# Weight sums of two seven-product block multiplications, built in HBM scratch by copies and accumulating DMAs

## The chip, the cores and the metric

One core of a Trainium2 chip runs the whole kernel. The metric is the device time of the program in microseconds (us), median of several runs. The profile is of one execution of the same program; its times are counted from the start of its span.

## The reference

One decoder layer on x (256 tokens, 2048 columns), float32. A combined projection `x @ w_in` gives latent queries, a latent key/value, gates, an indexer and a recurrent input. Branch A is sparse attention, branch B a gated linear recurrence (RG-LRU); each is gated and projected, then merged:

```
branch_a = (attn * silu(attn_gate)) @ w_branch_a
branch_b = (h * silu(rnn_gate)) @ w_branch_b
merged   = sigmoid(x @ w_gA) * branch_a + sigmoid(x @ w_gB) * branch_b
out      = layernorm(ALPHA * x + merged @ w_out) * g + b
```

All matrix products are float32. The kernel makes each from three products of a split pair: a value v is kept as hi (v rounded to the matmul's float32r) and lo = v - hi, and hi·hi + hi·lo + lo·hi is summed in PSUM.

## The kernel before

**Order of work.** `col_jobs()` lists column jobs in time order: index queries (qi), attention gates (ag), 32 query tiles (q), merge gate chunks ga and branch A chunks ba, recurrent inputs (xr), merge gate chunks gb, recurrent gates (rg). A chunk of 512 columns has 16 ticks, any other job 4. The hand-written list `TAIL` gives the rest: pieces of the branch B product (bb), of the output product (o), and steps t1, t2, t3. A tick is the unit of the kernel's own agenda: generators spawned at a tick (`spawn(t, gen)`) emit their next instructions there and name the number of ticks to the next turn. The order of emission is the order of each engine's queue; nothing is reordered later. `D0` is the tick of the first query job, `C0` that of the first recurrent input, `B0` the start of the tail.

**Weights.** All weight pieces are listed in `halves`, in the order of use. `load_to(n)` issues the loads up to piece n on SP's queue, each into a tile `raw` of 128x1024 float32 (a ring of 4). `split_to(n)` turns pieces into hi on ScalarE (`hi_of`, L151) and lo on VectorE (`lo_of`, L155), each a ring of 5. PE reads hi and lo. Loads are emitted about nine pieces ahead of use, splits about five.

**Seven-product steps.** In some places a 2x2 block product is made with seven block products instead of eight, which needs sums of weight blocks and of input blocks. Three such places exist:

- j (steps j1 to j4, beside the query jobs): two other column blocks; its sums stay as they are.
- s (steps s1 and s2, 8 each, inside the chunks ba 1, ba 2 and ba 3): the last column block of the first merge gate and the first of the second. Weight quarters 11, 12, 21, 22 are of 8 rows (k) of 128x512 each.
- t (steps t1, 4 of them, t2 and t3 in the tail): part of branch B's first two column blocks, quarters of 4 rows each.

Before the change the weight sums of s and t are made on VectorE, piece by piece: `load_to` fetches the pair of quarters of a row into one raw tile and a third quarter into a tile `form[k]` (s) or `t2` (t, which lies in the place of the first half of the normalised input `xs`, once that is no more needed). `sums(i)` and `split_to` then subtract: for s1a and t1a the lines 309 and 312 or 311, for s1b and t1b line 338, for s2a line 352, for t2 line 308. The pieces s1b, s2b and t1b have no raw tile of their own: they read what s1a and s2a left in theirs, or `form` and `t2`.

The input `xs` is kept as two tiles of half the rows behind a small class `Rows`, so that `t2` and later the merged rows (`m0`) can take the place of the first.

Other work on the queues that matters here: SP also loads the attention bias tiles (`load_bias`, from HBM scratch `dz`, L621), POOL adds the mask to them (L625), makes the late input sums of j (`late_sum`, L1017 to L1019) and issues its own DMAs: the copies `dz <- dv` of 1 MB from HBM to HBM (L612) and loads of input rows into `form` tiles (L949).

Of the kernel before, what the change touches and what calls it, by code (L numbers as in the profile page):

```python
# [11 lines left out]
F32 = mybir.dt.float32  # L12
# [81 lines left out]


def quarters(i):

    steps = [("j1", k) for k in range(8)] + [("j2", k) for k in range(8)]  # L100
    steps += [("j3", k) for k in range(4)] + [("j4", k) for k in range(8)]
    return steps[:1] if i == 3 else steps[i - 4:i - 3] if i > 4 else []


def ticks(job):

    return 16 if job[0] in CHUNKS else 4


class Rows:  # L110

    def __init__(self, parts):
        self.parts = parts

    def __getitem__(self, key):
        p, k, c = key
        if isinstance(k, slice):
            e = k.start // (KT // 2)
            return self.parts[e][p, k.start - e * (KT // 2):k.stop - e * (KT // 2), c]
        return self.parts[k // (KT // 2)][p, k % (KT // 2), c]  # L120


@with_exitstack
def layer(ctx, tc, ar, out):
# [89 lines left out]
    nc8 = const.tile([P, 16], F32, name="nc8")  # L214
    xs = Rows([big.tile([P, KT // 2, 2 * T], F32R, name=f"xs{e}", tag=f"xs{e}", bufs=1) for e in range(2)])
    dv = dram.tile([NH, VL], F32, name="dv")
# [26 lines left out]
    NZ = len(halves)  # L243
    halves += [("wo", 3, pc) for pc in range(8)]
    raws, parts = {}, {}
    st = {"load": 0, "split": 0}

    def load_to(n):
        while st["load"] < min(n, len(halves)):
            i = st["load"]  # L250
            kind, a, s = halves[i]
            st["load"] += 1
            if kind in ("s1b", "s2b", "t1b") or kind in ("j2", "j4") and a % 2:
                continue
            if kind == "s1a":
                nc.sync.dma_start(form[a], ar["wgb"][0, 4 + a // 2, :, a % 2, :])
            if kind == "t1a":
                if a == 0:
                    t2.append(big.tile([P, KT // 2, 2 * T], F32, name="t2", tag="xs0", bufs=1))
                nc.sync.dma_start(t2[0][:, a, :], ar["wbb"][1, (Q + a) // 2, :, (Q + a) % 2, :])  # L260
            raw = wpool.tile([P, 1024], F32, name=f"raw{i}", tag="raw", bufs=4)
            raws[i] = raw
            if kind == "t2":
                nc.sync.dma_start(raw[:, :512], ar["wbb"][0, (Q + a) // 2, :, (Q + a) % 2, :])
                continue
            if kind == "wt":
                src = ar["wt"][a, :, s * 8:(s + 1) * 8, :].rearrange("p k c -> p (k c)")
            elif kind == "j1":
                src = ar["wj"][a].rearrange("p k c -> p (k c)")
            elif kind in ("j2", "j3", "j4"):  # L270
                src = {"j2": ar["wgb"][3, 4 + a // 2], "j3": ar["wga"][2, a], "j4": ar["wga"][2, 4 + a // 2]}[kind]
                src = src.rearrange("p k c -> p (k c)")
            elif kind in ("s1a", "s2a"):
                src = ar["ws"][a + (8 if kind == "s2a" else 0)].rearrange("p k c -> p (k c)")
            elif kind == "t1a":
                src = ar["wbp"][a].rearrange("p k c -> p (k c)")
            elif kind == "t3":
                src = ar["wbb"][1, Q // 2 + a].rearrange("p k c -> p (k c)")
            else:
                src = ar[kind][a, s].rearrange("p k c -> p (k c)")  # L280
            nc.sync.dma_start(raw, src)
# [3 lines left out]
    form = {}  # L285
    t2 = []

    def sums(i):


        kind, k, _ = halves[i]
        if kind in ("j2", "j4") and k % 2:
            i = next(n for n in reversed(range(i)) if halves[n][:2] == (kind, k - 1))
        raw = raws[i]
        half = raw[:, k % 2 * 512:(k % 2 + 1) * 512]
        if kind == "j1":
            return nc.vector.tensor_sub(form[k], raw[:, 512:], raw[:, :512])
        if kind == "j2":
            return nc.vector.tensor_sub(form[k], half, form[k])
        if kind == "j3":  # L300
            for e in range(2):
                c = slice(e * 512, (e + 1) * 512)
                nc.vector.tensor_sub(raw[:, c], form[2 * k + e], raw[:, c])
            return
        if kind == "j4":
            return nc.vector.tensor_sub(form[k], form[k], half)
        if kind == "t2":
            return nc.vector.tensor_sub(raw[:, 512:], raw[:, :512], t2[0][:, k, :])
        nc.vector.tensor_sub(raw[:, 512:], raw[:, 512:], raw[:, :512])
        if kind == "t1a":  # L310
            return nc.vector.tensor_sub(t2[0][:, k, :], t2[0][:, k, :], raw[:, 512:])
        nc.vector.tensor_sub(form[k], form[k], raw[:, 512:])

    def split_to(n):
        while st["split"] < min(n, len(halves)):
            i = st["split"]
            kind, k, _ = halves[i]
            follower = halves[i + 1][0] if i + 1 < len(halves) else None
            if follower in ("s1a", "t1a"):
                load_to(i + 2)  # L320
                sums(i + 1)
            load_to(i + 1)
# [11 lines left out]
            else:  # L334
                if kind in ("s1b", "t1b"):
                    raw = raws.pop(i - 1)
                    v2 = form[k] if kind == "s1b" else t2[0][:, k, :]
                    nc.vector.tensor_sub(raw[:, 512:], v2, raw[:, :512])
                    src = [(slice(0, 512), v2), (slice(512, 1024), raw[:, 512:])]
                elif kind == "j1":  # L340
                    src = [(slice(0, 512), raws.pop(i)[:, :512]), (slice(512, 1024), form[k])]
                elif kind in ("j2", "j4"):
                    n = i if k % 2 == 0 else next(n for n in reversed(range(i)) if halves[n][:2] == (kind, k - 1))
                    raw = raws.pop(n) if k % 2 else raws[n]
                    src = [(slice(0, 512), raw[:, k % 2 * 512:(k % 2 + 1) * 512]), (slice(512, 1024), form[k])]
                elif kind == "s2b":
                    src = [(slice(0, 512), form[k])]
                else:
                    raw = raws[i] if kind in ("s1a", "t1a") else raws.pop(i)
                    src = [(slice(0, 1024), raw)]  # L350
                if kind == "s2a":
                    nc.vector.tensor_sub(form[k], form[k], raw[:, :512])
                hi = wpool.tile([P, 1024], F32R, name=f"hi{i}", tag="hi", bufs=5)
# [5 lines left out]
                parts[i] = (hi, lo)  # L359
            if follower in ("j1", "j2", "j3", "j4", "t2"):  # L360
                load_to(i + 2)
# [411 lines left out]
    def post_bb(i, pss):  # L773
# [10 lines left out]
        yield TURN[i]  # L784
        if i == 0:
            xs.parts[0] = big.tile([P, KT // 2, 2 * T], F32R, name="m0", tag="xs0", bufs=1)
        gs = [gates.pop(("gb", i, t)) for t in range(2)]
# [172 lines left out]
    def quarter_sums():  # L960
# [8 lines left out]
        for j in range(4):  # L969
# [4 lines left out]
                 for i, (tag, bufs) in enumerate((("g", 2), ("g", 2), ("u", 2), ("r", 3)))]  # L974
            nc.vector.tensor_add(v[0], a21, a22)
            nc.vector.tensor_sub(v[2], a11, a21)
            nc.vector.tensor_sub(v[1], v[0], a11)
            nc.vector.tensor_sub(v[3], a12, v[1])
            yield
# [146 lines left out]
    def after_s1():  # L1126
# [6 lines left out]
        yield  # L1133
        nc.vector.tensor_add(c22, ps7[5], u3)
        nc.vector.tensor_add(u4, ps7[5], u4)
        ps7["u"] = u1, u3, u4, c22

    def after_s2():

        u1, u3, u4, c22 = ps7["u"]  # L1140
        nc.vector.tensor_add(u1, ps7[2], u1)
        nc.vector.tensor_sub(u3, u3, ps7[4])
        for t in range(2):
# [11 lines left out]
    def branch_sums():  # L1155

        SB.update((i, sp.tile([P, 2, Q, P], F32R, name=f"sb{i}", tag="s", bufs=4)) for i in range(1, 5))
        for e in range(0, Q, 4):
# [3 lines left out]
            x = {1: v[:, b, P:], 2: v[:, a, :P], 3: v[:, a, P:], 4: v[:, b, :P]}  # L1162
            nc.vector.tensor_add(x[1], x[3], x[1])
            nc.vector.tensor_sub(x[3], x[2], x[3])
            yield
            nc.vector.tensor_sub(x[2], x[1], x[2])
            nc.vector.tensor_sub(x[4], x[4], x[2])
            yield
# [72 lines left out]
    def after_t1():  # L1241
# [8 lines left out]
        yield  # L1250
        nc.vector.tensor_add(u4, psb[5], u3)
        nc.vector.tensor_add(u2, psb[5], u2)
        spawn(t_now[0] + 8, load_norm(0))
# [5 lines left out]

    D0, C0, G0 = at["q", 0], at["xr", 0], at["gb", 1]  # L1260
    spawn(D0 - 30, early_sums())
    for j, t in enumerate((76, 79, 83, 87)):
# [335 lines left out]
def lay_out(x, w_in, kv_norm_g, w_uv, w_branch_a, conv_w, conv_b, w_gate_a, b_gate_a,  # L1598
# [14 lines left out]
    for kind, m in (("ga", w[:, O_GA:O_GA + DM]), ("gb", w[:, O_GB:O_GB + DM]),  # L1613
# [3 lines left out]
                         w[:, O_GB:O_GB + 512].reshape(KT, P, 512)], axis=2)  # L1617
    ar["wbp"] = w_branch_b[0, :Q * P].reshape(Q, P, 4, 512)[:, :, :2]
    ar["wj"] = np.stack([w[:DM // 2, O_GA + 2 * 512:O_GA + 3 * 512].reshape(KT // 2, P, 512),
# [27 lines left out]
```

## Time and profile before

| | |
|---|---|
| median of 3 runs | 1011.74 us (1011.54 to 1012.13) |
| the profiled execution, time | 1012.71 us |
| its span | 1010.9 us |
| mean granted TensorE clock | 0.998 |
| HBM read, written | 208.01 MB, 6.32 MB |

Each part of the profile is read so: busy time of an engine is the union of its instructions; a group of instructions has its count and minimum, median and maximum duration in ns; "idle before" and "waited for" name the event that came last before an engine went on. "q" behind an engine's name (SPq) is its queue of waits and DMA issues. "To landing" is the time from the issue of a DMA until its completion was signalled.

### The profile page before, as it was taken

Reading aid. Unit: us, or ns where it says so; the run is one execution under the profiler, and the core shown is the slowest. Engines: PE = TensorE matmul, PEld = TensorE weight load, DVE = VectorE, ACT = ScalarE, POOL = GpSimd, SP = SyncE. Lnnn points to the kernel's source line nnn. Section 1 sums busy time; section 2 is a strip of 40 time slices with the busy share of each in tenths; the row PEclk is TensorE's granted clock in tenths of the full one; section 3 lists DMA queues with packets and bytes.
Section 4 is the critical chain, followed back from the end, with each engine's and each line's share of the span. In section 5 each row is a group of like instructions: output and inputs, shape, how many; then the busy total and the mean of one; then the engine's idle time right before and its main releaser. Section 6 shows DMA issues by size and latency. Waiting matters only on the chain.

```text
span 1010.9 us, 15117 instructions
## 1 busy us (share of the span) xinstructions
PE 1002.9 (99%) x5308; PEld 864.7 (86%) x5308; DVE 810.5 (80%) x1340; ACT 605.5 (60%) x1037; POOL 153.0 (15%) x188
## 2 busy tenths in 40 slices
PE   9999999999999999999999999999999999999997
PEld 8888888888888888888888888888888888888885
DVE  5678789778789988868888878888678997978685
ACT  5566656666766576566455555555885555644452
POOL 0015621111123310210000000000343320001002
PEclk9999999999999999999999999999999999999999
DMA  9846886766656665766676776556556668667752
GB/s 301 264 150 196 282 324 198 234 216 197 188 157 208 198 201 164 231 210 208 206 232 204 213 233 190 186 191 198 172 180 191 190 198 289 205 201 264 226 173 84
DMA packets 65132, 211.14 MB, mean 209 GB/s; under 512 B 7184, under 2 KB 14224, under 8 KB 64288
## 3 DMA queue, kind: packets, MB, share of 16 engines
q1 hardware_dynamic: 61376, 196.37, 61.2%
q0 software_dynamic: 2960, 12.88, 3.6%
q8 instruction: 42, 0.69, 0.3%
q10 hardware_dynamic: 720, 0.92, 0.3%
q14 instruction: 34, 0.28, 0.1%
HBM read 208.01 MB, written 6.32 MB: 212 GB/s over the span
## 4 chain that ended last, share of the span: by engine, by line
PE 94%; DVE 3%; ACT 1%; issue 1%; DMA 1%; DVEq 0%; ACTq 0%
PE ps_q L368 17%; PE ps_ag L368 9%; PE ps_rg L368 9%; PE ps_xr L368 9%; PE ps_ba L1293 3%; PE ps_ba L1292 3%; PE ps_ba L1294 3%; PE psq L368 2%; PE ps_qi L368 2%; PE ps_o L1193 2%; PE ps_o L1191 2%; PE ps_o L1190 2%; PE ps_bb L1191 2%; PE ps_bb L1193 2%; PE ps_bb L1190 2%; PE ps_ga L1292 1%
## 5 line engine op out<-in xcount | busy, mean ns | idle before, releaser
L155 DVE TENSOR_TENSOR lo<-raw,hi 128x1024 fp32r<-128x1024 f32 (+1 forms) x354 | 420.0, 1194 | 154.4 <-ACT hi L151 150.3
L151 ACT ACTIVATE hi<-raw 128x1024 fp32r<-128x1024 f32 (+1 forms) x354 | 352.3, 1012 | 148.3 <-PE ps_q L368 16.7
L368 PE MATMUL ps_q<-xs,hi 128*128 128x512 f32 x512 | 126.9, 391 | 0.0
L368 PEld LDWEIGHTS ps_q<-xs,hi 128*128 128x128 f32 x512 | 94.0, 188 | 18.4
L368 PEld LDWEIGHTS ps_q<-xs,lo 128*128 128x128 f32 x512 | 65.6, 191 | 2.5
L368 PE MATMUL ps_q<-xs,lo 128*128 128x256 f32 x512 | 66.4, 283 | 0.0
L625 POOL TENSOR_TENSOR bias<-bias,mask 128x256 f32<-128x256 f32 (+1 forms) x32 | 33.0, 1050 | 195.4 <-DMA bias<-dz 182.7
L368 PE MATMUL ps_ag<-xs,hi 128*128 128x512 f32 x256 | 60.1, 391 | 0.0
L368 PE MATMUL ps_rg<-xs,hi 128*128 128x512 f32 x256 | 59.5, 390 | 0.0
L368 PE MATMUL ps_xr<-xs,hi 128*128 128x512 f32 x256 | 59.5, 390 | 0.0
L368 PEld LDWEIGHTS ps_xr<-xs,hi 128*128 128x128 f32 x256 | 47.6, 188 | 9.6
L368 PEld LDWEIGHTS ps_rg<-xs,hi 128*128 128x128 f32 x256 | 47.6, 188 | 9.6
L368 PEld LDWEIGHTS ps_ag<-xs,hi 128*128 128x128 f32 x256 | 47.5, 188 | 9.6
L1293 PE MATMUL ps_ba<-lo,ua 128*128 128x512 f32 x128 | 49.9, 389 | 0.0
L1294 PE MATMUL ps_ba<-hi,ua 128*128 128x512 f32 x128 | 49.8, 389 | 0.0
L1292 PE MATMUL ps_ba<-hi,ua 128*128 128x512 f32 x128 | 49.8, 389 | 0.0
L151 ACT ACTIVATE hi<-form 128x512 fp32r<-128x512 f32 x40 | 25.3, 633 | 28.8 <-PE ps_ba L1294 8.9
L1190 PE MATMUL ps_bb<-hi,ub 128*128 128x512 f32 x104 | 41.1, 395 | 0.0
L1193 PE MATMUL ps_bb<-hi,ub 128*128 128x512 f32 x104 | 40.6, 390 | 0.0
L1191 PE MATMUL ps_bb<-lo,ub 128*128 128x512 f32 x104 | 40.6, 390 | 0.0
L850 POOL MEMSET xp<- 128x3 f32 x16 | 1.5, 100 | 253.3 <-ACT ga L1150 163.9
L368 PE MATMUL ps_ag<-xs,lo 128*128 128x256 f32 x256 | 32.9, 283 | 0.0
(456 smaller groups left out, 2198.4 us busy)
## 6 DMA issues: line engine op xcount, KB each, us to landing
raw<-in_wt SPq DMA_DIRECT2D x168, 512.0 KB, 4.6
raw<-in_wba SPq DMA_DIRECT2D x32, 512.0 KB, 3.8
raw<-in_wo SPq DMA_DIRECT2D x32, 512.0 KB, 4.4
raw<-in_wbb SPq DMA_DIRECT2D x26, 512.0 KB, 4.2
raw<-in_wga SPq DMA_DIRECT2D x24, 512.0 KB, 4.5
raw<-in_wgb SPq DMA_DIRECT2D x20, 512.0 KB, 4.8
raw<-in_ws SPq DMA_DIRECT2D x16, 512.0 KB, 4.2
wr<-in_wA SPq DMA_DIRECT2D x14, 424.0 KB, 5.0
```

The source lines that it names most:

```text
L151: nc.scalar.activation(hi, src, AF.Copy)
L155: nc.vector.tensor_sub(lo, src, f(hi))
L368: nc.tensor.matmul(ps[:, :n], w, rhs[:, :n], start=start, stop=stop)
L625: nc.gpsimd.tensor_add(b[:, r, :W[r]], b[:, r, :W[r]], mask[:, r, :W[r]])
L850: nc.gpsimd.memset(xp[:, 0:3], 0.0)
L1190: nc.tensor.matmul(o, mh, hi, start=left[t] == left_of[key][t], stop=False)
L1191: nc.tensor.matmul(o, mh, lo, start=False, stop=False)
L1193: nc.tensor.matmul(o, ml, hi, start=False, stop=left[t] == 0)
L1292: nc.tensor.matmul(o, mh, hi, start=first and d == 0, stop=False)
L1293: nc.tensor.matmul(o, mh, lo, start=False, stop=False)
L1294: nc.tensor.matmul(o, ml, hi, start=False, stop=d == KT - 1)
```

## The change

The sums of s and t are made in HBM before they are needed. A generator `weight_sums` emits for each of four sums t1 = 11 (+) 12, t3 = 12 (+) 22, t2 = 11 (+) t3, t4 = 21 (+) t2 and each block of four rows one copy of the first operand into a scratch tile of 1 MB, on SP's queue, and one accumulating DMA of the second operand onto it, from POOL. Copy and add of one tile are two turns of nine ticks apart. The sums have plus signs only, so input sums and the final additions turn signs to match (an add for a subtract and the other way round, same number of instructions). The pieces s1a, s1b, s2a, s2b, t1a, t1b and t2 are then plain loads of one or two quarters of 256 KB, each into a raw tile of its own. `form` is no more loaded with weights for s, the tiles `t2` and `m0` go, and `xs` is one tile. The array `wbp` holds twice the rows.

```diff
+ROWS = 4
+PAIRS = {"s": "ws", "t": "wbp"}
+OPERANDS = {"s1a": ("11", "t1"), "s1b": ("t2", "t3"), "s2a": ("21", "22"), "s2b": ("t4",),
+            "t1a": ("11", "t1"), "t1b": ("t2", "t3"), "t2": ("21", "t4")}
...
-    xs = Rows([big.tile([P, KT // 2, 2 * T], F32R, name=f"xs{e}", tag=f"xs{e}", bufs=1) for e in range(2)])
+    xs = big.tile([P, KT, 2 * T], F32R, name="xs")
...
+    depth = {"s": KT // 2, "t": Q}
+    summed = {}
+
+    def quarter(p, n, k):
+        if n[0] == "t":
+            return summed[p, n, k // ROWS][:, k % ROWS, :]
+        return ar[PAIRS[p]][depth[p] * (n[0] == "2") + k, :, int(n[1]) - 1, :]
+
+    def several(p, n, k):
+        if n[0] == "t":
+            return summed[p, n, k]
+        r = depth[p] * (n[0] == "2") + ROWS * k
+        return ar[PAIRS[p]][r:r + ROWS, :, int(n[1]) - 1, :].rearrange("k p c -> p k c")
+
+    def weight_sums(p, gap):
+
+        begun = []
+        for n, first, second in (("t1", "11", "12"), ("t3", "12", "22"), ("t2", "11", "t3"), ("t4", "21", "t2")):
+            for k in range(depth[p] // ROWS):
+                d = summed[p, n, k] = dram.tile([P, ROWS, 512], F32, name=f"sum_{p}{n}_{k}")
+                nc.sync.dma_start(d, several(p, first, k))
+                begun.append((d, several(p, second, k)))
+                yield gap
+                if len(begun) > 1:
+                    add_rows(*begun.pop(0))
+        add_rows(*begun.pop())
+
+    def add_rows(d, src):
+
+        nc.gpsimd.dma_start(d, src, accum_op=OP.add, max_dma_last_dim=8192)
...
-            if kind in ("s1b", "s2b", "t1b") or kind in ("j2", "j4") and a % 2:
+            if kind in ("j2", "j4") and a % 2:
                 continue
-            if kind == "s1a":
-                nc.sync.dma_start(form[a], ar["wgb"][0, 4 + a // 2, :, a % 2, :])
...
-            if kind == "t2":
-                nc.sync.dma_start(raw[:, :512], ar["wbb"][0, (Q + a) // 2, :, (Q + a) % 2, :])
+            if kind in OPERANDS:
+                for e, part in enumerate(OPERANDS[kind]):
+                    nc.sync.dma_start(raw[:, e * 512:(e + 1) * 512], quarter(kind[0], part, a))
                 continue
...
-        if kind == "t2":
-            return nc.vector.tensor_sub(raw[:, 512:], raw[:, :512], t2[0][:, k, :])
-        nc.vector.tensor_sub(raw[:, 512:], raw[:, 512:], raw[:, :512])
-        if kind == "t1a":
-            return nc.vector.tensor_sub(t2[0][:, k, :], t2[0][:, k, :], raw[:, 512:])
-        nc.vector.tensor_sub(form[k], form[k], raw[:, 512:])
...
-                if kind in ("s1b", "t1b"):
-                    raw = raws.pop(i - 1)
-                    v2 = form[k] if kind == "s1b" else t2[0][:, k, :]
-                    nc.vector.tensor_sub(raw[:, 512:], v2, raw[:, :512])
-                    src = [(slice(0, 512), v2), (slice(512, 1024), raw[:, 512:])]
...
-                if kind == "s2a":
-                    nc.vector.tensor_sub(form[k], form[k], raw[:, :512])
...
-            nc.vector.tensor_add(v[0], a21, a22)
+            nc.vector.tensor_sub(v[0], a21, a22)
...
+    spawn(D0 + 40, weight_sums("s", 9))
+    spawn(C0 + 4, weight_sums("t", 9))
```

More of the change, by code (lines that the diff above doesn't have):

```diff
@@ L107, in ticks @@
     return 16 if job[0] in CHUNKS else 4
[L110 to L120, printed above, removed]
 @with_exitstack
@@ L252, in load_to @@
             st["load"] += 1
-            if kind in ("s1b", "s2b", "t1b") or kind in ("j2", "j4") and a % 2:
+            if kind in ("j2", "j4") and a % 2:
                 continue
-            if kind == "s1a":
-                nc.sync.dma_start(form[a], ar["wgb"][0, 4 + a // 2, :, a % 2, :])
-            if kind == "t1a":
-                if a == 0:
-                    t2.append(big.tile([P, KT // 2, 2 * T], F32, name="t2", tag="xs0", bufs=1))
-                nc.sync.dma_start(t2[0][:, a, :], ar["wbb"][1, (Q + a) // 2, :, (Q + a) % 2, :])
             raw = wpool.tile([P, 1024], F32, name=f"raw{i}", tag="raw", bufs=4)
             raws[i] = raw
-            if kind == "t2":
-                nc.sync.dma_start(raw[:, :512], ar["wbb"][0, (Q + a) // 2, :, (Q + a) % 2, :])
+            if kind in OPERANDS:
+                for e, part in enumerate(OPERANDS[kind]):
+                    nc.sync.dma_start(raw[:, e * 512:(e + 1) * 512], quarter(kind[0], part, a))
                 continue
@@ L272, in load_to @@
                 src = src.rearrange("p k c -> p (k c)")
[L273 to L276, printed above, removed]
             elif kind == "t3":
@@ L285, in layer @@
     form = {}
-    t2 = []
     def sums(i):
@@ L304, in sums @@
             return
-        if kind == "j4":
-            return nc.vector.tensor_sub(form[k], form[k], half)
-        if kind == "t2":
[L308 to L312, printed above, removed]
+        nc.vector.tensor_sub(form[k], form[k], half)
     def split_to(n):
@@ L318, in split_to @@
             follower = halves[i + 1][0] if i + 1 < len(halves) else None
-            if follower in ("s1a", "t1a"):
-                load_to(i + 2)
-                sums(i + 1)
             load_to(i + 1)
@@ L334, in split_to @@
             else:
-                if kind in ("s1b", "t1b"):
-                    raw = raws.pop(i - 1)
-                    v2 = form[k] if kind == "s1b" else t2[0][:, k, :]
-                    nc.vector.tensor_sub(raw[:, 512:], v2, raw[:, :512])
-                    src = [(slice(0, 512), v2), (slice(512, 1024), raw[:, 512:])]
-                elif kind == "j1":
+                if kind == "j1":
                     src = [(slice(0, 512), raws.pop(i)[:, :512]), (slice(512, 1024), form[k])]
@@ L345, in split_to @@
                     src = [(slice(0, 512), raw[:, k % 2 * 512:(k % 2 + 1) * 512]), (slice(512, 1024), form[k])]
-                elif kind == "s2b":
-                    src = [(slice(0, 512), form[k])]
-                else:
-                    raw = raws[i] if kind in ("s1a", "t1a") else raws.pop(i)
-                    src = [(slice(0, 1024), raw)]
-                if kind == "s2a":
-                    nc.vector.tensor_sub(form[k], form[k], raw[:, :512])
+                else:
+                    c = slice(0, 512 if kind == "s2b" else 1024)
+                    src = [(c, raws.pop(i)[:, c])]
                 hi = wpool.tile([P, 1024], F32R, name=f"hi{i}", tag="hi", bufs=5)
@@ L359, in split_to @@
                 parts[i] = (hi, lo)
-            if follower in ("j1", "j2", "j3", "j4", "t2"):
+            if follower in ("j1", "j2", "j3", "j4"):
                 load_to(i + 2)
@@ L784, in post_bb @@
         yield TURN[i]
-        if i == 0:
-            xs.parts[0] = big.tile([P, KT // 2, 2 * T], F32R, name="m0", tag="xs0", bufs=1)
         gs = [gates.pop(("gb", i, t)) for t in range(2)]
@@ L974, in quarter_sums @@
                  for i, (tag, bufs) in enumerate((("g", 2), ("g", 2), ("u", 2), ("r", 3)))]
-            nc.vector.tensor_add(v[0], a21, a22)
+            nc.vector.tensor_sub(v[0], a21, a22)
             nc.vector.tensor_sub(v[2], a11, a21)
             nc.vector.tensor_sub(v[1], v[0], a11)
-            nc.vector.tensor_sub(v[3], a12, v[1])
+            nc.vector.tensor_add(v[3], a12, v[1])
             yield
@@ L1133, in after_s1 @@
         yield
-        nc.vector.tensor_add(c22, ps7[5], u3)
-        nc.vector.tensor_add(u4, ps7[5], u4)
+        nc.vector.tensor_sub(c22, ps7[5], u3)
+        nc.vector.tensor_sub(u4, ps7[5], u4)
         ps7["u"] = u1, u3, u4, c22
@@ L1141, in after_s2 @@
         nc.vector.tensor_add(u1, ps7[2], u1)
-        nc.vector.tensor_sub(u3, u3, ps7[4])
+        nc.vector.tensor_add(u3, u3, ps7[4])
         for t in range(2):
@@ L1162, in branch_sums @@
             x = {1: v[:, b, P:], 2: v[:, a, :P], 3: v[:, a, P:], 4: v[:, b, :P]}
-            nc.vector.tensor_add(x[1], x[3], x[1])
+            nc.vector.tensor_sub(x[1], x[3], x[1])
             nc.vector.tensor_sub(x[3], x[2], x[3])
@@ L1166, in branch_sums @@
             nc.vector.tensor_sub(x[2], x[1], x[2])
-            nc.vector.tensor_sub(x[4], x[4], x[2])
+            nc.vector.tensor_add(x[4], x[4], x[2])
             yield
@@ L1250, in after_t1 @@
         yield
-        nc.vector.tensor_add(u4, psb[5], u3)
-        nc.vector.tensor_add(u2, psb[5], u2)
+        nc.vector.tensor_sub(u4, psb[5], u3)
+        nc.vector.tensor_sub(u2, psb[5], u2)
         spawn(t_now[0] + 8, load_norm(0))
@@ L1617, in lay_out @@
                          w[:, O_GB:O_GB + 512].reshape(KT, P, 512)], axis=2)
-    ar["wbp"] = w_branch_b[0, :Q * P].reshape(Q, P, 4, 512)[:, :, :2]
+    ar["wbp"] = w_branch_b[0, :2 * Q * P].reshape(2 * Q, P, 4, 512)[:, :, :2]
     ar["wj"] = np.stack([w[:DM // 2, O_GA + 2 * 512:O_GA + 3 * 512].reshape(KT // 2, P, 512),
```

## The prediction

> **What bounds the kernel now.** I read the page first (shares and chain), then the waits of PE, then the stages that the change touches in a table of windows.
>
> ```profile
> span 1010.9 us, 15117 instructions
> PE 1002.9 (99%) x5308; PEld 864.7 (86%) x5308; DVE 810.5 (80%) x1340; ACT 605.5 (60%) x1037; POOL 153.0 (15%) x188
> PE 94%; DVE 3%; ACT 1%; issue 1%; DMA 1%; DVEq 0%; ACTq 0%
> ```
>
> TensorE is busy for all but 8.0 us of the span and makes 94% of the chain. A busy PE could hide short stalls, so the waits of PE come next, all that the view lists:
>
> ```profile
> PE warm L381 <- DVE eps L205: 1.0, 1, 1.0
> PE psn L1519 <- ACT mrow L151: 0.4, 1, 0.4
> PE pspT L702 <- DVE vl L155: 0.4, 1, 0.4
> PE pm L1516 <- DVE mcol L1513: 0.3, 1, 0.3
> PE psm L793 <- DVE gb L782: 0.2, 1, 0.2
> ```
>
> They sum to 2.3 us, of which 1.0 is the start and 0.7 (psn, pm) the end. Only the last row lies near a part that changes. The stages (columns: length, busy us and count for each engine, granted clock, DMA share, GB/s):
>
> ```profile
> 119.00:145.00 26.00, 26.00 (x148) 22.77 (x148) 21.58 (x61) 15.13 (x24) 11.40 (x15) 1.00 1.00 367
> 305.00:410.00 105.00, 104.64 (x598) 91.38 (x597) 91.71 (x178) 69.47 (x150) 22.02 (x22) 1.00 0.63 198
> 471.00:551.00 80.00, 80.00 (x354) 66.22 (x353) 68.78 (x87) 42.16 (x51) 0.00 (x0) 1.00 0.72 220
> 551.00:592.00 41.00, 41.00 (x182) 33.88 (x182) 33.11 (x38) 21.69 (x24) 0.00 (x0) 1.00 0.71 211
> 842.00:880.00 38.00, 38.00 (x172) 31.29 (x171) 32.51 (x40) 23.05 (x30) 0.00 (x0) 1.00 0.70 225
> 880.00:915.00 35.00, 34.82 (x160) 28.56 (x159) 27.71 (x34) 17.04 (x18) 1.07 (x2) 1.00 0.64 207
> ```
>
> 471 to 551 is the s1 stage, 551 to 592 the s2 stage, 842 to 880 holds the t1 steps, 880 to 915 the t2 steps, 305 to 410 the query projections beside which the new sums would be built. PE is full in all of them, but for 0.18 us in the t2 stage. VectorE, which is relieved, is at 0.86 (68.78 of 80) in s1 and holds nobody up.
>
> **What is removed.** The subtractions on VectorE that built the sums:
>
> ```profile
> L309 DVE TENSOR_TENSOR raw<-raw x12: 683/684/687, 478.5 to 870.2; 128x512 f32<-128x512 f32 x12
> L312 DVE TENSOR_TENSOR form<-form,raw x8: 691/692/695, 479.2 to 536.7; 128x512 f32<-128x512 f32 x8
> L338 DVE TENSOR_TENSOR raw<-form,raw x8: 691/692/694, 482.2 to 540.5; 128x512 f32<-128x512 f32 x8
> L352 DVE TENSOR_TENSOR form<-form,raw x8: 683/686/687, 545.8 to 581.9; 128x512 f32<-128x512 f32 x8
> L311 DVE TENSOR_TENSOR t<-t,raw x4: 692/692/693, 851.4 to 870.9; 128x512 f32<-128x512 f32 x4
> L338 DVE TENSOR_TENSOR raw<-t,raw x4: 685/692/692, 855.7 to 873.9; 128x512 f32<-128x512 f32 x4
> L308 DVE TENSOR_TENSOR raw<-raw,t x4: 683/684/687, 887.7 to 898.7; 128x512 f32<-128x512 f32 x4
> ```
>
> That is 48 instructions of about 0.69 us, 33 us of VectorE: 22 us in s1 and s2, 11 us in t1 and t2. PE stays the bound in s1, s2 and t1 (idle 0.00), so 22 us and most of the 11 return nothing. In t2 the idle 0.18 us may go. Gain: 0.2 us; at most 0.6 us, if the wait of pspT, in the query stage, went too. The products on PE are the same in number and form, the turned signs swap an add for a subtract of the same shape, and the one undivided xs only drops a change of tile between t2 and the merged rows: nothing for these.
>
> **What is added, first place: copies and adds of 1 MB.** For s there are 4 sums of 2 blocks, for t 4 sums of 1 block: 12 copies on SP's queue and 12 accumulating DMAs from POOL, one of each every 9 ticks, s from tick 40 of the query jobs, t from tick 4 of the recurrent inputs. The nearest rows, a 1 MB copy from HBM to HBM, and what pays for a tick:
>
> ```profile
> L621 SPq DMA_DIRECT2D bias<-dz x16: 385/426/1394, 178.0 to 421.0; - x16
> L612 POOL DMA_DIRECT2D dz<-dv x4: 547/572/598, 102.4 to 135.1; - x4
> ...
> DMA to landing us min/median/max: 4.4/5.8/8.9
> raw<-in_wt SPq DMA_DIRECT2D x8, 512.0 KB, 7.4
> dz<-dv POOLq DMA_DIRECT2D x2, 1024.0 KB, 8.6
> ```
>
> The first three are of the tile dz, the last two the DMA view of 119 to 140 us. The biases are loaded every 8 ticks, 15 steps in 243.0 us, so a tick is 2.03 us and 9 ticks 18.2 us. One 1.05 MB copy per 18.2 us is 58 GB/s and an add priced as the same copy 58 more: 198 + 116 = 314 GB/s, under the 367 GB/s at which 119 to 145 us ran with PE at 26.00 of 26.00 although raw loads took 7.4 us to land. What covers this is the ring of four raw tiles:
>
> ```profile
> raw<-in_wt SPq DMA_DIRECT2D x22, 512.0 KB, 4.3
> raw<-in_wga SPq DMA_DIRECT2D x12, 512.0 KB, 5.0
> raw<-in_wuv SPq DMA_DIRECT2D x1, 512.0 KB, 5.3
> SPq L281 <- DVE lo L155: 79.2, 34, 5.9
> ```
>
> (305 to 410 us, DMA and the waits of SP.) 35 raw loads in 105 us are 3.0 us each, so a tile of the ring may take 12 us from issue to return. With a landing of 7.4 us and a conversion of about 2.4 us (below) it takes 9.8. I take nothing. If the cover goes, the excess of the landing over 9.6 us counts, a quarter of it per load. POOL issues an add in 0.57 us by the dz row; what stands behind it there is the bias sum and the late sums, which have the next head's time. An add waits for a copy issued 18 us before, and t2's add for t3's add 36 us before, against 8.9 us for the slowest dz: no wait. SP's copies wait for nothing, cost an issue each, and stand ahead of the raw loads in SP's queue, where SP itself waits 79.2 of 105 us for VectorE to return tiles. Neither bound of an accumulating DMA is in the trace: below, it costs no more than a copy; above, I let it double the traffic.
>
> A rule of the Trainium skill speaks against this change: in "Collectives: The Full Stack", section "The bandwidth ceiling: the fold count and why AG ≠ RS ≠ AR", a reducing DMA reads two sources for one write and so loads the read side twice as much as a copy. By it the stage would run at an estimated 198 + 58 + 116 = 372 GB/s, just the load of 119 to 145 us, and the sum would still get nothing; no run here shows an accumulating DMA.
>
> **What is added, second place: raw tiles and loads.** Before, s1b, s2b and t1b took no raw tile; now each step of two weights loads two quarters of 256 KB into a raw tile of its own. SP has 56 quarter loads instead of 24 loads in s, and 24 instead of 12 in t, each an issue of 0.33 us, beside its waits. The ring of four decides in s2, where there will be three raw tiles (s2a, s2b, ba) for two:
>
> ```profile
> 559.90 0.33 SPq L281 DMA_DIRECT2D raw<-in_ws  x1
> 562.93 0.33 SPq L281 DMA_DIRECT2D raw<-in_wba  x1
> 560.58 2.01 ACT L151 ACTIVATE hi<-raw 128x1024 fp32r<-128x1024 f32 x2 [0.73 <-PE ps L1117]
> 563.98 0.63 ACT L151 ACTIVATE hi<-form 128x512 fp32r<-128x512 f32 x1 [1.39 <-PE ps_ba L1294]
> 565.34 2.01 ACT L151 ACTIVATE hi<-raw 128x1024 fp32r<-128x1024 f32 x2 [0.73 <-PE ps L1117]
> 561.68 1.23 DVE L155 TENSOR_TENSOR lo<-raw,hi 128x1024 fp32r<-128x1024 f32 x1
> raw<-in_wba SPq DMA_DIRECT2D x6, 512.0 KB, 3.8
> raw<-in_ws SPq DMA_DIRECT2D x5, 512.0 KB, 4.1
> form<-in_wgb SPq DMA_DIRECT2D x8, 256.0 KB, 5.1
> ```
>
> (Timelines of SP, ScalarE and VectorE, and DMA of 551 to 592 us; the last row is of the page.) The period is 565.34 − 560.58 = 4.76 us. The conversion of a full tile takes from 560.58 to 561.68 + 1.23 = 562.91, 2.33 us, and SP issues into the tile at 562.93. A ba tile's life will be 3.8 + 0.1 + 2.33 = 6.2 us, s2a's 0.33 + 4.1 + 0.1 + 2.33 = 6.9, s2b's, half converted (0.63 + 0.69), 4.1 + 0.1 + 1.4 = 5.6. The sum of the three is 18.7, and with four tiles in turn a period takes a quarter of it, 4.7 us: just the 4.76 that PE takes. With the quarters at 5.1 us it is 20.7, 5.2 us a period, 0.4 us late in each of 8: 3.3 us in all. The cover: ScalarE waits for PE's five hi tiles now. A converted piece is needed 4/3 of a period later, 6.35 us, less 2.0 + 1.23: about 3.1 us ahead; and ws issued at 559.90 lands by 564.0 where its hi, second of the two, starts at 566.3: 2.3 us more. 5.4 us cover 3.3, so again nothing. I take the lower values, nearest in shape and stage. Upper end: all landings at 7.4 us, sum 29.2, 7.3 us a period, 8 × 2.5 − 5.4 = 14.9 us.
>
> In s1 four tiles have 36 matmuls, at 41.00/182 = 0.225 us each 8.1 us; lives 6.2, 6.9, 6.9, 6.2 sum to 26.2, 6.6 us: hidden. In t1 (24 matmuls, 5.4 us) 6.2 + 6.9 + 6.9 give 5.0 and with 5.1 us quarters 5.5: hidden. In t2 the number of raw tiles stays; each loses a subtraction and gains a quarter load. This is late next there: the landing of two quarters, by the same lives no later than now.
>
> **Sum.** The profiled execution took 1012.71 us, 1.8 more than its span, 1.0 above the median 1011.74. Against itself: −0.2 + 0 + 0 = 1012.5; against the median 1011.5.
>
> **Rivals.** (1) PE covers all: 1011.5 us. For it: PE without idle, 5.4 us cover. (2) The raw ring starves PE in s2. It decides when the period's sum passes 22.7 us (8 × 0.91 = 5.4 + 2 us), landings about 1.3 us over those taken. For it: s2's traffic grows from 1.05 to 1.31 MB per 4.76 us, 220 to 275 GB/s, and 7.4 us landings at 367; against: 3.8 to 4.1 at 211. At landings of 6 us (sum 25.0) it loses 8 × 1.49 − 5.4 = 6.5 us: 1018. (3) The accumulating DMAs crowd the query stage: landings of 12 us beside them make 14.4 us lives, 0.6 us late for each of some 35 loads, 21 us less a cover like that of s2: 1027; for half of them 1017. Against: 8.9 us for the slowest dz. (4) VectorE's 33 us return: more than 2.0 us would need more than all of PE's 2.3 us of waits but 0.3, while 1.7 are at start and end.
>
> **Numbers.** 0.2% (2.0 us) is about what a measurement can tell. (1) 0.67, (2) 0.21, (3) 0.09, (4) 0.03: same 0.67, slower 0.30, faster 0.03. Range 1010.8 (all of the 0.6 us, and 0.3 for the spread of the runs) to 1018.0 (rival 2 at 6 us landings); above lie the rest of (2) and most of (3). The likeliest case alone: 1010.8 to 1013.5.
>
> **What would show it.** Right: the 48 subtractions gone, VectorE 777 us, PE waits still about 2 us, SP waiting for VectorE in s2 and landings near 4.1. Wrong: ScalarE's hi waiting for DMA in s2 and PE below 41 us of its stage (2); landings over 9.6 us between 240 and 400 us with PE gaps (3); fewer PE waits and a shorter span (4). What would break the working: an add that holds POOL for many microseconds, or scratch loads that land later than inputs.

## The result, and the profile after

The changed kernel takes 1019.06 us (median of 4 runs, 1018.09 to 1019.66) against 1011.64 us before: ratio 1.0072, 95% interval 1.0055 to 1.0089. That is 7.4 us slower, where no change was forecast and the range ended at 1018.0. The profiled execution is the fastest of the four, 1018.09 us with a span of 1016.3 us, 5.4 us over the span before, so the profile shows 5.4 of the 7.4 us.

The page after: the span, the shares, the DMA queues and the chain.

```profile
span 1016.3 us, 15185 instructions
PE 1003.7 (99%) x5308; PEld 863.5 (85%) x5308; DVE 784.8 (77%) x1280; ACT 605.0 (60%) x1025; POOL 163.4 (16%) x200
q1 hardware_dynamic: 74048, 215.25, 63.7%
q0 software_dynamic: 6992, 25.46, 10.4%
PE 88%; DVE 5%; DMA 4%; ACT 1%; issue 1%; DVEq 0%; ACTq 0%
```

VectorE has 25.7 us less of busy time than before, and the time still rose. The chain, which was PE to 94%, now has 4% of DMA and 5% of VectorE in it. PE's waits say where (all rows of over 0.3 us):

```profile
PE pspT L697 <- DVE vl L148: 2.7, 2, 2.3
PE pspT L697 <- ACT lg L694: 1.8, 2, 1.3
PE warm L376 <- DVE eps L198: 1.0, 1, 1.0
PE psj L1047 <- DVE gb L1075: 0.4, 1, 0.4
PE psn L1514 <- ACT mrow L144: 0.4, 1, 0.4
```

The start and the end are as before. What is new is pspT, the transposes of an attention head in the query stage: 4.5 us for 0.4. The stages (columns as before; the query stage, then s1, s2 and the t stages, which lie 5 us later now):

```profile
235.00:305.00 70.00, 70.00 (x408) 61.73 (x407) 55.84 (x111) 46.45 (x100) 15.02 (x14) 1.00 0.88 267
305.00:345.00 40.00, 37.24 (x210) 31.95 (x209) 35.91 (x59) 22.18 (x47) 15.92 (x15) 1.00 0.92 279
345.00:425.00 80.00, 77.62 (x435) 66.40 (x434) 65.34 (x140) 51.29 (x113) 12.06 (x16) 1.00 0.88 266
476.00:556.00 80.00, 80.00 (x355) 66.20 (x354) 52.49 (x56) 41.78 (x44) 0.00 (x0) 1.00 0.78 242
556.00:597.00 41.00, 41.00 (x182) 33.81 (x181) 27.55 (x30) 21.23 (x24) 0.00 (x0) 1.00 0.75 248
847.00:885.00 38.00, 38.00 (x172) 31.30 (x171) 25.00 (x24) 22.98 (x26) 0.00 (x0) 1.00 0.78 258
885.00:920.00 35.00, 35.00 (x160) 28.93 (x159) 29.30 (x32) 17.51 (x19) 1.09 (x2) 1.00 0.78 250
```

Nearly all of it is lost in 305 to 425 us: 2.76 + 2.38 us without PE, where before it was 0.36 us from 305 to 410. That is 4.8 of the 5.4 us. In s1, s2 and t1 PE is full as before, and the 0.18 us of t2 came back. The stage that loses is the second part of the one beside which the sums are built (in the first part, 235 to 305 us, PE stays full beside three of the adds); the stages that use the sums lose nothing. The bytes alone don't tell of it: 266 to 279 GB/s, below the 314 that were worked out, at a DMA share of 0.88 to 0.92 where it was 0.63 before. Its DMA rows, from 305 to 424 us (POOL's queue and the loads of raw tiles, before and then after):

```profile
q0 software_dynamic: 160, 0.52, 1.2%
raw<-in_wt SPq DMA_DIRECT2D x22, 512.0 KB, 4.3
DMA to landing us min/median/max: 3.5/4.5/6.6
```

```profile
q0 software_dynamic: 1473, 5.97, 26.7%
raw<-in_wt SPq DMA_DIRECT2D x22, 512.0 KB, 6.8
DMA to landing us min/median/max: 3.5/6.5/11.6
ACT hi L144 <- DMA raw<-in_wt: 19.7, 9, 4.8
```

A raw tile lands in 6.5 us for 4.5 in the median, and in 11.6 at most. The last row is new altogether: in this stage ScalarE stands 19.7 us before a hi whose raw tile hasn't landed. Before, no such wait is listed there. The chain through the worst place (start, duration, what; and PE's stall at its end from the timeline):

```profile
302.30 7.54 DMA raw<-in_wt
309.92 1.07 ACT hi L144
...
312.27 6.49 DMA raw<-in_wt
...
319.40 2.00 ACT hi L144 x2
...
325.91 1.16 DVE vl L148 x2
327.16 0.33 PE L697 MATMUL pspT<-ident,lg 128*128 128x128 f32 x1 [2.31 <-DVE vl L148]
```

A load of 7.5 us, its hi, a tile returned, the next load of 6.5 us, and then VectorE's work in order, in which `vl` stands behind the late splits. PE needs the PSUM bank that `vl` reads. It does not stop for a weight piece but for the head's work behind the pieces.

### The profile page after: what moved, and what is told of

Same layout as the page of the kernel before. It is cut to its first block, busy times and chain, and to the rows that moved or that the text cites. A ratio compares the mean times of both kernels' runs of the same rounds, so it can differ in the third digit from the quotient of the medians.

```text
span 1016.3 us, 15185 instructions
## 1 busy us (share of the span) xinstructions
PE 1003.7 (99%) x5308; PEld 863.5 (85%) x5308; DVE 784.8 (77%) x1280; ACT 605.0 (60%) x1025; POOL 163.4 (16%) x200
## 4 chain that ended last, share of the span: by engine, by line
PE 88%; DVE 5%; DMA 4%; ACT 1%; issue 1%; DVEq 0%; ACTq 0%
PE ps_q L363 11%; PE ps_ag L363 9%; PE ps_xr L363 9%; PE ps_rg L363 9%; DMA raw<-in_wt 3%; PE ps_ba L1287 3%; PE ps_ba L1288 3%; PE ps_ba L1289 3%; PE ps_bb L1186 2%; PE ps_bb L1183 2%; PE ps_bb L1184 2%; PE psq L363 2%; PE ps_qi L363 2%; PE ps_o L1183 2%; PE ps_o L1186 2%; PE ps_o L1184 2%
## 5 line engine op out<-in xcount | busy, mean ns | idle before, releaser
L148 DVE TENSOR_TENSOR lo<-raw,hi 128x1024 fp32r<-128x1024 f32 (+1 forms) x362 | 433.0, 1203 | 184.9 <-ACT hi L144 182.5
L144 ACT ACTIVATE hi<-raw 128x1024 fp32r<-128x1024 f32 (+1 forms) x362 | 364.5, 1018 | 182.1 <-DMA raw<-in_wt 35.3
L1183 PE MATMUL ps_o<-hi,xs 128*128 128x512 f32 x96 | 37.6, 391 | 0.0
L1186 PE MATMUL ps_o<-hi,xs 128*128 128x512 f32 x96 | 37.4, 389 | 0.0
```

Of the source, the lines that this page charges most:

```text
L144: nc.scalar.activation(hi, src, AF.Copy)
L148: nc.vector.tensor_sub(lo, src, f(hi))
L1183: nc.tensor.matmul(o, mh, hi, start=left[t] == left_of[key][t], stop=False)
L1186: nc.tensor.matmul(o, ml, hi, start=False, stop=left[t] == 0)
```

## The experiments

Each ratio is to the kernel before, run beside it on the same chip. Theory A at the start is that the traffic of the sums makes raw loads late in the query stage. Rival B is that the additional raw tiles and quarter loads cost the time, where the sums are used.

**No sums at all** (`e3_no_sums`):

```diff
-            return summed[p, n, k // ROWS][:, k % ROWS, :]
+            n = {"t1": "12", "t2": "21", "t3": "22", "t4": "12"}[n]
...
-    spawn(D0 + 40, weight_sums("s", 9))
-    spawn(C0 + 4, weight_sums("t", 9))
```

> All copies and adds are left out; the quarters that would be read from the scratch sums are read from the input quarters instead (so the products use other weights); raw tiles, quarter loads and the relieved VectorE stay as in the changed kernel. Theory A (the traffic of copies and adds beside the query jobs makes raw loads land late, and PE stalls there): the 7 us are gone, 1011 to 1012 us, PE full in the query stage. Rival B (the raw ring and the quarter loads of s1, s2, t1 cost it): still 1017 to 1019 us.

1011.80 us, ratio 1.0006 (0.9997 to 1.0014): the loss is gone with all raw tiles and quarter loads of the change in place. B falls. It also shows what the freed VectorE gives if the sums cost nothing: no gain.

**The kernel before with the sums of s beside it** (`e4_before_with_s_sums`): `weight_sums` and its helpers put into the kernel before, and

```diff
+    spawn(D0 + 40, weight_sums("s", 9))
```

> The kernel before, with the copies and adds of s issued beside its query jobs at the same ticks into scratch that nothing reads. Theory A: the loss is there without any of the rest, 1016 to 1019 us, PE idle between 305 and 425 us. Rival B: 1011.5 to 1012 us, since the raw ring is that of before.

1017.26 us, ratio 1.0053 (1.0040 to 1.0066): 5 to 6 of the 7 us, from DMAs that nothing waits for. In its profile PE has 37.73 of 40 and 76.25 of 79 us in 305 to 424. A holds; the 1 to 2 us that are left for the sums of t are within the two intervals.

**Copies without adds** (`e1_no_adds`):

```diff
-        nc.gpsimd.dma_start(d, src, accum_op=OP.add, max_dma_last_dim=8192)
+        pass
```

> The accumulating DMAs are left out, the copies stay (so the sums lack their second operand). Theory A1 (the copies, which stand in the same queue ahead of the raw loads, make the lateness): most of the loss stays, 1015 to 1018 us. Theory A2 (the adds, which land in 11.6 us against 9.4 us of a copy, make it): 1011.5 to 1013 us. If it is the sum of both: about 1013 to 1015 us. Rival B: 1017 to 1019 us.

1011.18 us, ratio 1.0001 (0.9992 to 1.0010). The copies alone cost nothing that can be measured, though they stand in SP's queue right in front of raw loads. So the loss needs the adds (theory A2); adds without copies were not run.

**Plain DMAs in the adds' place** (`e2_copies_for_adds`):

```diff
-        nc.gpsimd.dma_start(d, src, accum_op=OP.add, max_dma_last_dim=8192)
+        nc.gpsimd.dma_start(d, src, max_dma_last_dim=8192)
```

> Each accumulating DMA is replaced by a plain DMA of the same source and destination from the same queue (so the second operand overwrites the first). Theory that an accumulating DMA loads the engines as two reads and a write: less than the changed kernel, 1013 to 1016 us, landing 8 to 9 us for 11.6. Theory that its bytes count like a copy's: no change, 1017 to 1019 us. Rival B: no change.

1012.91 us, ratio 1.0014 (1.0006 to 1.0023): a loss of 1.8 us, not 7, and a touch less than expected. POOL's queue and the raw landings from 305 to 424 us:

```profile
q0 software_dynamic: 1103, 6.09, 13.8%
DMA to landing us min/median/max: 3.4/5.6/9.1
```

The same 6 MB on the same queue keep the 16 engines busy for 13.8% of the window as plain DMAs and for 26.7% as accumulating ones: 1.9 times. Of the 7.4 us, about 1.8 remain with plain DMAs of the same bytes, and the rest comes with accumulating.

Now the mechanism between a late raw tile and PE. Theory C is that PE only stops at pspT, where the head has too little time. Rival D is that conversion as a whole falls behind.

**Transposes later** (`e6_transpose_later`):

```diff
-        yield 3
+        yield 5
         ps = aux_tile(f"pspT{h}")
...
-        yield 5
+        yield 3
         g, e = divmod(h, 4)
```

> The changed kernel with a head's transposes (pspT) emitted two ticks later (yield 5 for 3) and the value products at their old tick (3 for 5), about 4 us more between the end of a head's softmax and PE's need of it. Theory C (PE does not stop for late weights, but at pspT, because ScalarE and VectorE work in order and the softmax stands behind a hi that waits for its raw tile): most of the 7 us come back, 1012 to 1014.5 us, no waits of pspT. Rival D (the weight pieces themselves arrive too late): still 1017 to 1019 us, the stalls move to other products.

1017.84 us, ratio 1.0065 (1.0052 to 1.0078). pspT no longer waits, but other products do, and from 305 to 424 us PE is idle for 4.7 us, nearly as in the changed kernel (5.1):

```profile
PE pspv L714 <- DVE pa L148: 2.5, 2, 1.4
PE ps_xr L363 <- ACT hi L144: 1.7, 2, 1.2
PE psj L1047 <- DVE gb L1075: 1.3, 1, 1.3
```

C falls. pspT was only the first to meet a backlog on ScalarE and VectorE.

**Five raw tiles** (`e7_five_raw`):

```diff
-            raw = wpool.tile([P, 1024], F32, name=f"raw{i}", tag="raw", bufs=4)
+            raw = wpool.tile([P, 1024], F32, name=f"raw{i}", tag="raw", bufs=5)
```

> The changed kernel with five raw tiles for four. Loads start one tile earlier, some 3 us in the query stage. If the late landing works through the ring's cover, in either theory C or D: 1012 to 1015 us, ScalarE's waits for raw tiles in the query stage mostly gone. If the engines that move data are simply full there: no change, 1017 to 1019 us.

1012.67 us, ratio 1.0010 (1.0001 to 1.0019): 6 of the 7 us come back, with the accumulating DMAs where they were. From 305 to 424 us:

```profile
q0 software_dynamic: 1614, 6.45, 27.6%
DMA to landing us min/median/max: 4.1/7.8/13.9
ACT hi L144 <- DMA raw<-in_wt: 6.5, 3, 2.8
305.00:345.00 40.00, 39.36 (x221) 33.97 (x221) 35.80 (x63) 24.70 (x52) 18.14 (x15) 1.00 0.98 300
345.00:424.00 79.00, 79.00 (x453) 69.24 (x452) 66.50 (x146) 52.34 (x116) 11.37 (x16) 1.00 0.93 284
```

The landings are longer still, 7.8 us, and yet ScalarE waits 6.5 us for 19.7, and PE is idle for 0.6 us, for 0.4 before the change (the profiled execution, 1011.39 us, is the fastest of this kernel). So the engines that move data are not the bound; the ring's depth against the landing is. POOL isn't either: it issues the same adds here.

**The sums of s earlier** (`e5_s_sums_earlier`), before the part in which VectorE is fullest:

```diff
-    spawn(D0 + 40, weight_sums("s", 9))
+    spawn(D0 - 16, weight_sums("s", 8))
```

> The sums of s begin 56 ticks earlier (tick D0 - 16, a turn every 8), so that they are done by about 300 us, before the part of the query stage in which VectorE is at 0.87 and more. Theory E (what counts is that VectorE has no slack between 305 and 420 us): 1011.5 to 1013.5 us. If the traffic costs the same wherever it lies beside the jobs: 1016 to 1019 us. As the traffic is a little denser (8 ticks for 9), a loss of its own before 300 us may remain.

1028.35 us, ratio 1.0170 (1.0156 to 1.0185): far worse, against the expectation. From 305 to 424 us PE is full but for 0.05 us; the loss has moved with the sums:

```profile
160.00:235.00 75.00, 68.12 (x382) 58.91 (x381) 49.85 (x88) 41.01 (x78) 10.22 (x12) 0.98 1.02 301
235.00:305.00 70.00, 65.53 (x367) 56.53 (x366) 51.85 (x108) 44.15 (x98) 7.27 (x11) 0.98 0.87 265
```

VectorE had 61 of 75 us there in other runs (61.44 in the one with later transposes), so a VectorE as full as from 305 us on isn't needed for a loss, and theory E as it stood falls. But the run is also denser. Ticks are shorter in that part, the first two adds start 14 us apart, all of them 18.0 us apart in the mean, where the changed kernel has 20.7, and the DMA share from 160 to 235 us is 1.02, for 0.70 in the run with later transposes. The granted clock of 0.98 in these two windows would be about 2.9 us of the loss; whether it has to do with the change stays open.

**The same, thinner** (`e11_thinner`): a turn every 14 ticks from D0 − 16.

```diff
-    spawn(D0 + 40, weight_sums("s", 9))
+    spawn(D0 - 16, weight_sums("s", 14))
```

> The changed kernel with the sums of s begun at D0 - 16 as in the run of them earlier, but a turn every 14 ticks, so that they end where they did: the same DMAs over a longer time. If the mean load decides: 1011.5 to 1014 us. If each 1 MB add costs its stall wherever it falls among query jobs: 1017 us or more.

1014.84 us, ratio 1.0039 (1.0025 to 1.0052), a little above the interval that a mean load would give and well below the other. With the same bytes, adds 18.0, 20.7 and 30.5 us apart (8, 9 and 14 ticks a turn) give losses of 17.0, 7.4 and 3.4 us; their places differ too, so this is no curve of the rate alone. Where the thin adds cost something says more:

```profile
160.00:235.00 75.00, 75.00 (x432) 66.10 (x431) 61.42 (x110) 49.45 (x94) 12.76 (x13) 1.00 0.93 288
235.00:305.00 70.00, 70.00 (x411) 61.82 (x410) 55.03 (x108) 46.11 (x101) 11.03 (x13) 1.00 0.85 263
305.00:345.00 40.00, 38.90 (x217) 33.34 (x216) 36.36 (x64) 23.50 (x50) 18.30 (x15) 1.00 0.81 252
345.00:424.00 79.00, 77.53 (x436) 67.13 (x436) 66.87 (x143) 53.39 (x117) 13.65 (x14) 1.00 0.75 223
```

Beside the first five adds, from 160 to 305 us, PE stays full; beside the last three, two of them issued together, it is idle for 2.6 us (0.4 before), at a smaller DMA share. VectorE is busy for 0.82 and 0.79 of the first two windows, for 0.91 and 0.85 of the last two. So adds cost more where VectorE has less slack. That fits theory E as a part of the account, but isn't shown, as no run changed VectorE's load alone.

**Single rows** (`e8_one_row_each`): copies and adds of 256 KB, one of each every 2 ticks.

```diff
-ROWS = 4
+ROWS = 1
...
-    spawn(D0 + 40, weight_sums("s", 9))
-    spawn(C0 + 4, weight_sums("t", 9))
+    spawn(D0 + 40, weight_sums("s", 2))
+    spawn(C0 + 4, weight_sums("t", 2))
```

> The same copies and adds cut into single rows of 256 KB, one copy and one add every 2 ticks: same bytes, a quarter of the size, about the same rate. If single bursts of 1 MB in front of a raw load make the lateness: 1012 to 1015 us, raw landings with a lower maximum. If the mean load makes it: 1016 to 1020 us; each of 48 adds also costs POOL about 0.7 us.

1014.04 us, ratio 1.0034 (1.0022 to 1.0047): 4 to 5 us better than whole blocks, at a slightly higher rate. So bursts of 1 MB count as well as the mean. In this run the adds waited for their copies, 26 times and 90 us in all on POOL; whether that made any of what is left was not tested.

**Is it the fifth tile itself?** Three runs with `bufs=5` as above: the kernel before with nothing else, the kernel before with the unread sums of s, and the changed kernel with single rows.

> The kernel before with five raw tiles for four, nothing else. Theory F (the fifth tile only gives cover for late landings): no change, 1010.5 to 1012 us, as PE has nothing to get back. Rival (the fifth tile is worth something by itself, so that it says nothing of the sums): 1 us or more faster.

> The kernel before with the copies and adds of s beside its query jobs, unread, and five raw tiles. Theory F: the 6 us that the same kernel with four tiles loses come back, 1011 to 1013 us, with raw landings as late as there. Rival (the fifth tile helped the changed kernel in s2, where three raw tiles stand for two): still 1016 to 1018 us.

> The changed kernel with copies and adds of one row of 256 KB and five raw tiles, the two that helped together. Theory F: PE full in the query stage, 1010.5 to 1012 us, no faster than before by more than 1 us, because without any sums it was not faster either. If VectorE's 33 us were worth something once the loads are in time: under 1010 us.

1011.25 us, ratio 1.0000 (0.9991 to 1.0009); 1012.17 us, 1.0008 (0.9999 to 1.0017); 1011.50 us, 1.0002 (0.9993 to 1.0011). All three are as theory F has it (the fifth tile only gives cover for late landings): it is worth nothing by itself, takes back about 5 of the 6 us of unread sums, and with finer adds the change costs nothing measurable. It also gains nothing. No version beats the kernel before.

## Why the prediction was wrong

**Right.** PE bounds; the 33 us of subtractions return nothing (1.0006 without any sums), and the 0.18 us of t2 went. VectorE came to 784.8 us for the 777 forecast (779.5 without the sums), which cost nothing. The raw ring of s2 came out nearly as worked out. It was to be the late one and just covered; after the change ScalarE's waits in 556 to 597 us are

```profile
ACT hi L144 <- DMA raw<-in_wba: 5.7, 6, 2.0
ACT hi L144 <- DMA raw<-in_ws: 2.4, 3, 1.2
ACT hi L144 <- DMA raw<-sum_st: 2.0, 1, 2.0
```

so the ring does set the pace of conversion, and PE is full (41.00 of 41) on the pieces already made. Quarter loads landed in 4.0 and 4.3 us, near the 4.1 taken, but those of ba in 5.1 us for 3.8. By the forecast's own sum that is 20.1 us for the three tiles, about 2 us late over the stage, inside the 5.4 us of cover. POOL took up to 1.3 us to issue an add for the 0.57 taken, and nothing waited for its bias sums. An add was to wait for nothing; among the sums of t one waited 2.9 us for its copy, at no visible cost. Three sums are a little off without touching the result: by its own lives the three tiles make 24.7 and 28.9 us at landings of 6 and 7.4 us, not 25.0 and 29.2, and t1's 5.5 us is not quite hidden behind 5.4.

**The step that failed** is the first place of what is added: "With a landing of 7.4 us and a conversion of about 2.4 us (below) it takes 9.8. I take nothing." Its result was that landings have to pass 9.6 us before anything is lost. The loss came at 6.5 us in the median. Two terms were wrong:

1. The cover was one mean for all tiles. The conversion of a plain piece was sized well: paired in order in the timelines of ScalarE and VectorE from 305 to 424 us, the full pieces (36 before, 34 after) take 2.5 us in the median from the start of the hi to the end of the lo, though the longest takes 5.5 us before and 6.4 after. What the forecast left out stands in the profile before (rows of the timelines of ScalarE and VectorE):

```profile
347.61 0.65 ACT L151 ACTIVATE hi<-raw 128x512 fp32r<-128x512 f32 x1
356.12 0.62 ACT L151 ACTIVATE hi<-raw 128x512 fp32r<-128x512 f32 x1
358.75 0.69 DVE L155 TENSOR_TENSOR lo<-raw,hi 128x512 fp32r<-128x512 f32 x1
```

Both hi read one raw tile, a half each, for two steps j4 that stand beside two query jobs. The tile is held from 347.61 until 359.44, 11.8 us for the 2.4 taken; three more of the 40 tiles of this window are held for 9 to 10 us, and four whose sums are made in place for 4 to 5. The turns of the pieces are uneven as well. Before the change, the time from a tile's landing to its first reader is 3.8 us in the median, but under 1.2 us for 7 of the 40 tiles, which have no 2 us to give. (From 235 to 305 us, where the adds cost nothing, the least is 1.7 us, though tiles are held for 9 to 11 us there too.) After the change it is 1.5 us in the median, and 16 of 36 tiles have a reader that begins within 0.5 us of the landing, for 2 of 40 before and 8 of 39 with five raw tiles. In the mean the forecast's rule still finds cover: a landing of 6.7 us and 3.9 us from first reader to return make 10.6 of the 12 us. So the mean was the wrong measure. How much of the loss is due to the tiles that are held, to the uneven turns and to single landings of up to 11.6 us was not separated. SP's 79 us of waiting for tiles did leave it room to issue the copies (the run without adds bears that out), but the same row says that the ring was always in use. That landings of 7.4 us were borne from 119 to 145 us was no proof for this stage: all tiles there are plain pieces.

2. In the sum the add was priced at a copy's traffic, with twice of it as the upper bound. It keeps the engines busy 1.9 times as long, near that bound. The rule on two reads for one write, of the Trainium skill's "Collectives: The Full Stack" (section "The bandwidth ceiling: the fold count and why AG ≠ RS ≠ AR"), agrees with what this case's runs show, 26.7% against 13.8% for 6 MB. The runs show the factor and not its reason, as the adds also went out in more packets (1473 for 1103 on that queue). The rule had been set aside because the sum came out the same by it, which rested on the first error.

The rival that came true is the third, "the accumulating DMAs crowd the query stage", with 0.09. Its place and sign were right (1017 us for half of the loads late, 1027 for all), its mechanism nearly: landings late, but to 6.5 us and not 12. Its point of decision was set too far away by the mean. The fault of the forecast was to give the stage with the added traffic a cover worked out from an even ring and from a conversion in another stage, without looking at the tiles of this one.

**Open.** Why adds every 8 ticks cost 17 us and every 9 ticks 7.4 was not settled; both overrun the ring, but they lie beside different parts of the query stage.

## What to carry to other kernels

Before moving work into DMAs that run "beside" a stage, take the life of each load buffer from that stage's own rows, from issue to the last reader's end, and compare the growth of the landing with the least room between a landing and its first reader, not with the mean; an in-order engine that stands before a tile not yet landed delays all that is queued behind it, so PE may stop at something that has no link to the load. Price an accumulating DMA as two transfers (1.9 here). If such traffic must stay, small pieces and one more load buffer took back nearly all of it here, but work taken off an engine that PE does not wait for gave nothing.

## What the runs showed of the hardware

Accumulating DMAs from HBM to HBM (1 MB, float32, runs of 2 KB) landed in 11.6 us in the median for 7.6 us of a plain DMA of the same shape from the same queue, and POOL was busy 1.17 us with the issue of one for 0.71 us (the groups of the sums' tiles, the changed kernel and then the one with plain DMAs). With a scratch tile as the source it was 11.7 for 9.4 us:

```profile
L267 POOL DMA_DIRECT2D sum_st<-in_ws x4: 1141/1169/1262, 262.5 to 330.2; - x4
sum_st<-in_ws POOLq DMA_DIRECT2D x4, 1024.0 KB, 11.6
```

```profile
L267 POOL DMA_DIRECT2D sum_st<-in_ws x4: 702/708/733, 263.1 to 329.6; - x4
sum_st<-in_ws POOLq DMA_DIRECT2D x4, 1024.0 KB, 7.6
```

Copies of 1 MB on SP's queue, right before raw loads in the same queue, moved the raw landings only from 4.5 to 4.7 us in the median and cost no time.
